# State-space outputs copied out of their PSUM banks by ScalarE, both in one step, and retention's offsets made by GpSimd

## The chip, the cores and the metric

The kernel runs on one core of one Trainium2 chip. The metric is the device time in microseconds (us) of one execution: the kernel before was run three times, and one further execution was recorded by the hardware profiler. Its rows are what the prediction reads. PE is TensorE (the matrix engine), ACT is ScalarE, DVE is VectorE, POOL is GpSimd, SP is SyncE, which issues most transfers.

## The reference

A trunk of two layers runs on two groups of 1024 tokens with 1024 channels. Layer 0 is the one that the change touches. One input projection feeds retention heads and state-space (S5) groups side by side; each is gated, and one output projection follows:

```python
z = h @ w_in
q, k, v, ga, ub, gb = jnp.split(z, [...], axis=-1)
o_a = _head_norm(_retention(q, k, v.reshape(hs))).reshape(B, L, D_RET) * jax.nn.silu(ga)
...
def _head_norm(o):
    mu = jnp.mean(of, axis=-1, keepdims=True)
    var = jnp.mean(jnp.square(of - mu), axis=-1, keepdims=True)
    return ((of - mu) * lax.rsqrt(var + EPS)).astype(o.dtype)
...
def _s5(u, ...):                     # 32 groups of 16 channels, 64 complex states each
    y = _s5_scan(... forward) + _s5_scan(... backward)
    y = y.reshape(B, L, D_SSM) + d_skip.astype(jnp.float32) * uf
    y = jax.nn.gelu(y)
    y = y * jax.nn.sigmoid(y @ w_glu.astype(jnp.float32))
```

Layer 1 is neighbourhood attention with its own projections. The change does not touch it.

## The kernel before

Every projection is made from matrices split into a high and a low part, so that one product takes three matmuls (wh·hh, wh·hl, wl·hh; `dense`, L259). `project` (L238) walks over column blocks of the weights in two halves of 512 tokens, 24 matmuls each, into bank d of PSUM. After each half it calls `unit()` (L183), which lets every background task take one step: the S5 task (`s5`, L824), one retention task per head and group (`ret_mix`, L972), and others. TensorE's instructions keep the order in which the program issues them, so the projection's matmuls fill the time between the small matmuls of the tasks. The order on the other engines is set by the framework's scheduler, and then each engine works its list off in order.

PSUM has eight banks here (L1367): two for d, and one each for a, b, c, z, y and e. A bank is written again only when the last reader of what it held is done.

S5 runs in 16 rounds, one per pair of groups g0 and g1, with four steps each (L839 to L857). Step 1: `s5_states` of g0 (four matmuls into bank z; two DVE products L790 and L791, a POOL sum L792, four DVE scans L795, two DVE products L796 and L797, a POOL sum L798), the output of the last pair's g1, and `s5_begin` of the next pair (POOL, L688 and following). Step 2: `s5_states` of g1. Step 3: `s5_place` of g0 (two ACT copies of the scanned states into `xs`) and `s5_tables` of the next pair (DVE). Step 4: `s5_place` of g1, `s5_matrices` of the next pair (PE into banks e and z, ACT copies), and the output of g0.

An output (`s5_out`, L807) is three matmuls into bank y and then the first form of gelu: ACT squares the bank into y2 (L816), DVE makes (y2 + 1)·y (L817, reads the bank), ACT takes the tanh (L818), DVE makes (tanh + 1)·y into g2 (L820, reads the bank again), and two stores take g2 away. So bank y is held from the first matmul to the end of L820, and g0 of a pair and g1 of it use it in neighbouring steps.

A retention head's `outputs` (L1016) sums into bank b (or another), takes mean and variance on DVE, makes the inverse root brs in two instructions (`rsqrt`: DVE L206, POOL L207, a power), and then the offset bnb = -mean·brs on DVE (L1034). One step later `normal` (L1037) runs four ACT activations (L1040) with brs as scale and bnb as offset into `on`, `finish` transposes it, multiplies by the gate (L1048) and stores it to oD. In the memory map, region A8 has one slot for `on` and one for `sd` (the scores times the decay, which `outputs` uses up).

## Time and profile before

| | us |
|---|---|
| median of 3 runs (lowest to highest) | 2236.64 (2235.96 to 2238.22) |
| the profiled execution's own time | 2242.2 |
| its span, first to last instruction | 2240.4 |
| PE, DVE, ACT, POOL busy in it | 2175.2, 1307.2, 962.3, 752.0 |

S5 and retention are active from about 150 to 900 us of the span, the output projection of layer 0 follows to about 1112 us, then layer 1. The mean granted TensorE clock is 0.988 of full. A row of the trace names line, engine, operation, output and inputs; "[2.07 <-DVE E L820]" means that the engine sat idle for 2.07 us and that the DVE instruction of line 820, which writes to region E, ended that. A name such as psy is bank y, E and A are regions of SBUF.

### The profile page before, as it was taken

The page shows a single profiled execution, that of the slowest core. Times are in us where ns is not written, and L with a number is a line of the kernel's source. Part 1 is how long each engine was busy: PE and PEld are TensorE (multiplying, and loading weights), DVE is VectorE, ACT ScalarE, POOL GpSimd, SP SyncE. Part 2 cuts the span into 40 slices and gives each one's busy share as a digit, 9 for nine tenths or more (in the row PEclk, how much of TensorE's full clock was granted, in tenths as well). Part 3 has the DMA queues.
Part 4 walks back from the last instruction along what each step waited for, and adds up shares of the span by engine and source line. Part 5 has one row for each costly group of instructions (what it writes and reads, how often), then busy time and mean ns, then how long its engine had stood idle before and what let it go on. Part 6 is the DMA issues. An engine that isn't in the chain of part 4 may idle for free.

```text
span 2240.4 us, 35109 instructions
## 1 busy us (share of the span) xinstructions
PE 2175.2 (97%) x13248; PEld 1830.9 (82%) x13248; DVE 1307.2 (58%) x2865; ACT 962.3 (43%) x2114; POOL 752.0 (34%) x646
## 2 busy tenths in 40 slices
PE   7999999998999999999999999999999999999998
PEld 4668778876878888888989898888888898987886
DVE  4736777878787556475434545457555555457322
ACT  4634434434443444243344444447444445355211
POOL 2544355557464120355611111113111212113333
PEclk9999999999999999999999999999999999999999
DMA  9993322224212245535521112124111111115454
GB/s 333 287 272 95 92 75 46 71 72 125 67 56 59 83 148 172 177 129 169 163 69 52 51 40 63 45 69 100 55 55 50 45 55 55 55 41 159 113 139 123
DMA packets 292640, 231.12 MB, mean 103 GB/s; under 512 B 54392, under 2 KB 263672, under 8 KB 292472
## 3 DMA queue, kind: packets, MB, share of 16 engines
q1 hardware_dynamic: 289016, 220.51, 33.2%
q10 hardware_dynamic: 3456, 8.39, 1.0%
q8 instruction: 104, 1.70, 0.3%
q14 instruction: 64, 0.52, 0.1%
HBM read 169.92 MB, written 56.84 MB: 101 GB/s over the span
## 4 chain that ended last, share of the span: by engine, by line
PE 77%; DVE 8%; DMA 7%; POOL 3%; issue 3%; ACT 3%; SPq 1%; DVEq 0%; ACTq 0%; POOLq 0%
PE psd L131 56%; PE psc L131 5%; PE psa L131 5%; PE psb L136 4%; DMA out_y<-h_lo 4%; PE psb L131 2%; PE psz L131 2%; DVE E L795 2%; PE psy L131 2%; DMA oD<-A 1%; PE psa L136 1%; DMA wr<-in_w_in_ab 1%; ACT h_hi L202 1%; DVE A L688 1%; PE pse L131 1%
## 5 line engine op out<-in xcount | busy, mean ns | idle before, releaser
L131 PE MATMUL psd<-h_hi,wh 128*128 128x512 f32 x1392 | 554.1, 398 | 3.0 <-DVE A L879 3.0
L131 PE MATMUL psd<-h_lo,wh 128*128 128x512 f32 x1392 | 547.3, 393 | 0.6 <-DVE h_lo L476 0.4
L131 PE MATMUL psd<-h_hi,wl 128*128 128x512 f32 x1392 | 545.6, 392 | 0.0
L131 PEld LDWEIGHTS psd<-h_hi,wh 128*128 128x128 f32 x1392 | 263.2, 189 | 59.3 <-DVE A L879 3.5
L131 PEld LDWEIGHTS psd<-h_hi,wl 128*128 128x128 f32 x1392 | 262.7, 189 | 55.9 <-issue 0.4
L131 PEld LDWEIGHTS psd<-h_lo,wh 128*128 128x128 f32 x1392 | 263.0, 189 | 55.4 <-issue 2.9
L131 PE MATMUL psd<-wh,h_hi 128*128 128x256 f32 (+1 forms) x960 | 279.5, 304 | 3.0 <-DVE A L946 2.0
L131 PE MATMUL psd<-wl,h_hi 128*128 128x256 f32 (+1 forms) x864 | 251.3, 291 | 0.1
L202 ACT ACTIVATE wh<-wr 128x1024 fp32r<-128x1024 f32 x118 | 124.7, 1058 | 244.6 <-PE psd L131 132.6
L213 POOL TENSOR_TENSOR wl<-wr,wh 128x1024 fp32r<-128x1024 f32 x51 | 126.5, 2480 | 262.3 <-ACT wh L202 230.3
L131 PE MATMUL psd<-wh,h_lo 128*128 128x256 f32 x768 | 213.7, 278 | 0.0
L131 PEld LDWEIGHTS psd<-wh,h_hi 128*128 128x128 f32 x960 | 181.0, 189 | 12.0 <-DVE A L946 2.4
L131 PEld LDWEIGHTS psd<-wl,h_hi 128*128 128x128 f32 x864 | 162.6, 188 | 3.9 <-POOL wl L213 0.5
L1236 POOL TENSOR_TENSOR A<-A,A 128x256 f32<-128x256 f32 (+1 forms) x80 | 56.5, 727 | 264.7 <-DVE nm L1254 260.0
L131 PEld LDWEIGHTS psd<-wh,h_lo 128*128 128x128 f32 x768 | 145.0, 189 | 0.3
L213 DVE TENSOR_TENSOR wl<-wr,wh 128x1024 fp32r<-128x1024 f32 x67 | 87.4, 1306 | 72.2 <-ACT wh L202 72.1
L1256 ACT ACTIVATE E<-E,nm 128x368 f32<-128x368 f32 (+1 forms) x172 | 98.0, 571 | 52.0 <-DVE nm L1254 51.8
L395 DVE TENSOR_TENSOR rs<-ss 128x1 f32<-128x1 f32 x64 | 42.2, 660 | 116.5 <-ACT h_lo L1153 56.4
L1274 DVE COPY A<-psb 128x384 f32<-128x384 f32 x64 | 33.5, 523 | 122.5 <-PE psb L136 121.3
L688 POOL TENSOR_TENSOR A<-A 128x288 f32<-128x288 f32 (+1 forms) x128 | 92.8, 745 | 30.9 <-DVE E L736 22.1
L131 PE MATMUL psd<-ow,oh 128*128 128x512 f32 x320 | 101.4, 396 | 1.0 <-ACT oh L202 1.0
L1236 POOL TENSOR_TENSOR A<-A 128x368 f32<-128x368 f32 x16 | 13.9, 891 | 254.3 <-DVE nm L1254 253.7
(351 smaller groups left out, 4409.7 us busy)
## 6 DMA issues: line engine op xcount, KB each, us to landing
wr<-in_w_in_c SPq DMA_DIRECT2D x64, 512.0 KB
wr<-in_w_in_ab SPq DMA_DIRECT2D x48, 512.0 KB
wr<-oD SPq DMA_DIRECT2D x32, 512.0 KB
wn<-in_w_mod SPq DMA_DIRECT2D x24, 512.0 KB
wm<-in_w_mod SPq DMA_DIRECT2D x8, 1024.0 KB
ox<-in_x SPq DMA_DIRECT2D x16, 512.0 KB
x1D<-ox SPq DMA_DIRECT2D x16, 512.0 KB
oD<-E SPq DMA_DIRECT2D x32, 256.0 KB
```

Source lines behind the costliest of these rows:

```text
L131: i = self.nc.tensor.matmul(*a, **k)
L136: i = self.nc.tensor.transpose(*a, **k)
L202: self.nc.scalar.activation(dst, src, AF.Copy, scale=scale)
L213: e.tensor_tensor(lo, raw, hi.bitcast(F32), SUB)
L395: self.nc.vector.tensor_tensor(rs, ss[:, 0:1], ss[:, 1:2], ADD)
L688: eng.tensor_tensor(dst, x.unsqueeze(3).to_broadcast(sh), y.unsqueeze(2).to_broadcast(sh), op)
L795: Vv.tensor_tensor_scan(t1[:, q], r8, t1[:, q], 0.0, MUL, ADD)
L1236: self.nc.gpsimd.tensor_tensor(b, raw[a][:, c0:c0 + n], mask, ADD)
L1256: nc.scalar.activation(sn, sn, AF.Exp, bias=nm, scale=-1.0, accum_out=su)
L1274: self.nc.vector.tensor_copy(pt, pp)
```

## The change

- **The memory map.** A8 holds two slots of `sd`. `on` is gone: `outputs` hands its `sd` on, and `normal` writes over it.
- **S5's outputs.** After the square (now L818) ACT also copies the bank into g2 (`copy_a`, L202; yc is a view of g2). Both DVE products, L820 (in place of L817) and L827 (in place of L820), read SBUF alone. g0's output goes to bank y and g1's to bank e. Both outputs of a pair are issued in step 1 of the next round, and the new `s5_gelu` (tanh L826, second product L827, stores) in step 2. The loop has a 17th, partial round for the last pair.
- **Placing.** Both `s5_place` calls stand in step 4 (g0's stood in step 3), and the copies into bm moved from `s5_tables` (step 3) to `s5_matrices` (step 4).
- **Retention's offset.** DVE makes bnb = -mean (L1047) before the root, and POOL multiplies it by brs (L1049) after the power.

```diff
-    "A7 qf 2048 qb 2048; A8 sd 2048 on 2048; A9 vfb 2048 th 2048; A10 rt1 2048 rt2 2048")
+    "A7 qf 2048 qb 2048; A8 sd 2048 sd 2048; A9 vfb 2048 th 2048; A10 rt1 2048 rt2 2048")
...
     def s5_out(self, st, g):
-        x, gi = self.xs[g], 2 * st["pi"] + g
-        ys = self.pst("y")[:, 0:256]
+        x = self.xs[g]
+        ys = self.pst("ye"[g])[:, 0:256]
...
         y2 = self.t([P, 256], "y2")
+        g2 = self.t([P, 2, P], "g2")
+        yc = g2.rearrange("p s c -> p (s c)")
         nc.scalar.activation(y2, ys, AF.Square, scale=0.044715 ** 0.5)
-        Vv.scalar_tensor_tensor(y2, y2, 1.0, ys, ADD, MUL)
+        self.copy_a(yc, ys)
+        Vv.scalar_tensor_tensor(y2, y2, 1.0, yc, ADD, MUL)
+        st["y"][g] = y2, g2, yc
+
+    def s5_gelu(self, st, g):
+        nc, Vv, gi = self.nc, self.nc.vector, 2 * st["pi"] + g
+        y2, g2, yc = st["y"][g]
         nc.scalar.activation(y2, y2, AF.Tanh, scale=G0)
-        g2 = self.t([P, 2, P], "g2")
-        Vv.scalar_tensor_tensor(g2.rearrange("p s c -> p (s c)"), y2, 1.0, ys, ADD, MUL)
+        Vv.scalar_tensor_tensor(yc, y2, 1.0, yc, ADD, MUL)
...
-        for pi in range(16):
-            self.s5_states(st, 0)
-            if pi:
-                self.s5_out(last, 1)
+        last = None
+        for pi in range(17):
+            if st:
+                self.s5_states(st, 0)
+            if last:
+                for g in range(2):
+                    self.s5_out(last, g)
             nx = self.s5_begin(pi + 1) if pi < 15 else None
             yield
-            self.s5_states(st, 1)
+            if st:
+                self.s5_states(st, 1)
+            if last:
+                for g in range(2):
+                    self.s5_gelu(last, g)
+            if not st:
+                return
             yield
-            self.s5_place(st, 0)
             if nx:
                 self.s5_tables(nx)
             yield
-            self.s5_place(st, 1)
+            for g in range(2):
+                self.s5_place(st, g)
             if nx:
                 self.s5_matrices(nx)
-            self.s5_out(st, 0)
             last, st = st, nx
             yield
-        self.s5_out(last, 1)
...
+            Vv.tensor_scalar(nb, mv[:, :, 0], -1.0, None, MUL)
             self.rsqrt(rs, mv[:, :, 1], 4, 1.0, EPS)
-            Vv.scalar_tensor_tensor(nb, mv[:, :, 0], -1.0, rs, MUL, MUL)
-            return po3, rs, nb
-
-        def normal(po3, rs, nb):
-            on = self.t([P, 4, P], "on")
+            G.tensor_tensor(nb, nb, rs, MUL)
+            return po3, rs, nb, sd
+
+        def normal(po3, rs, nb, on):
```

Three places show how the lists of the engines move. On TensorE, step 4 of the first round before (psy_1797 is the output of g0, from the states placed just ahead; pse_1768 and psz_1774 are the next pair's matrices):

```order
L136 MATMUL pse_1768<-ident,E_183_1345 128x128 x4
L131 MATMUL psz_1774<-A_192_1397,A_184_1346 48x144 x2
L131 MATMUL psz_1774<-A_184_1346 48x144 x2
L131 MATMUL psy_1797<-E_193_1410,E_198_1454 128x256
L131 MATMUL psy_1797<-E_183_1345,A_192_1397 128x256
L131 MATMUL psy_1797<-E_183_1345,A_184_1346 128x256
L131 MATMUL pse_1807<-sel,A_191_1395 128x2
```

and step 1 of the next round in the changed kernel (psz_1854 are the states of the next pair's g0; psy_1869 and pse_1876 are the outputs of g0 and g1):

```order
L131 MATMUL psz_1854<-E_193_1410 64x256 x4
L131 MATMUL psy_1869<-E_193_1410,E_198_1454 128x256
L131 MATMUL psy_1869<-E_183_1345,A_192_1397 128x256
L131 MATMUL psy_1869<-E_183_1345,A_184_1346 128x256
L131 MATMUL pse_1876<-E_193_1410,E_198_1454 128x256
L131 MATMUL pse_1876<-E_183_1345,A_192_1397 128x256
L131 MATMUL pse_1876<-E_183_1345,A_184_1346 128x256
L131 MATMUL pse_1900<-wr_1724,cs 32x128 x8
L136 MATMUL psa_1915<-ident,kT_1570 128x128 x4
```

The three matmuls of g0's output moved from behind psz's matrices to behind psz's states, a step later; the three of g1's output kept their place and changed their bank. Nothing else moved on TensorE.

On ScalarE, the same place about the fourth round (psb_2998 in the first list and psb_3000 in the second are the same retention output). Before:

```order
L816 ACTIVATE A_184_1346<-psy_2961 128x256
L202 ACTIVATE A_191_1395<-pse_2988 128x128
L818 ACTIVATE A_184_1346<-A_184_1346 128x256
L202 ACTIVATE wh_3051<-wr_3050 128x1024
L202 ACTIVATE A_213_1571<-psd_3025 64x512 x2
L202 ACTIVATE E_183_1345<-E_217_1595 64x4x127 x2
L1040 ACTIVATE A_257_2086<-psb_2998,bnb_3013,brs_3012 128x128 x4
```

and now:

```order
L818 ACTIVATE E_198_1454<-psy_2959 128x256
L202 ACTIVATE E_198_1454<-psy_2959 128x256
L818 ACTIVATE A_184_1346<-pse_2966 128x256
L202 ACTIVATE E_198_1454<-pse_2966 128x256
L826 ACTIVATE E_198_1454<-E_198_1454 128x256
L202 ACTIVATE A_191_1395<-pse_2990 128x128
L826 ACTIVATE A_184_1346<-A_184_1346 128x256
L202 ACTIVATE E_183_1345<-E_217_1595 64x4x127 x2
L202 ACTIVATE wh_3054<-wr_3053 128x1024
L202 ACTIVATE A_213_1571<-psd_3028 64x512 x2
L1054 ACTIVATE A_257_2084<-psb_3000,bnb_3015,brs_3014 128x128 x4
```

Two squares with a copy each stand together, the two tanh follow with one copy between them, and the copies of scanned states (E_183) moved ahead of the weight cast wh; the four activations of the normalisation stand behind all of these in both lists.

On VectorE, that retention output's statistics and offset. Before (L1034 is the offset, L790 and L791 the next state products):

```order
L797 TENSOR_TENSOR E_217_1595<-E_217_1595,E_198_1454 128x512
L1032 BN_AGGR bmv_3011<-bst_3010 128x2 x4
L206 TENSOR_SCALAR brs_3012<-bmv_3011 128x4
L790 TENSOR_TENSOR E_217_1595<-psz_3061,E_198_1454 128x512
L791 TENSOR_TENSOR E_217_1595<-psz_3061,E_183_1345 128x512
L371 TENSOR_TENSOR mods<-pse_3076,bmod 128x2
L1034 SCALAR_TENSOR_TENSOR bnb_3013<-bmv_3011,brs_3012 128x4
L946 TENSOR_TENSOR A_213_1571<-psd_3025,cosT_1538 128x512
L947 TENSOR_TENSOR A_213_1571<-A_213_1571,sinT_1540 128x512
```

and now (L1047 is -mean):

```order
L827 SCALAR_TENSOR_TENSOR E_198_1454<-E_198_1454 128x256
L796 TENSOR_TENSOR E_217_1595<-E_217_1595,E_183_1345 128x512
L827 SCALAR_TENSOR_TENSOR E_198_1454<-A_184_1346,E_198_1454 128x256
L797 TENSOR_TENSOR E_217_1595<-E_217_1595,E_198_1454 128x512
L1045 BN_STATS bst_3012<-psb_3000 128x6 x4
L1046 BN_AGGR bmv_3013<-bst_3012 128x2 x4
L1047 TENSOR_SCALAR bnb_3015<-bmv_3013 128x4
L206 TENSOR_SCALAR brs_3014<-bmv_3013 128x4
L790 TENSOR_TENSOR E_217_1595<-psz_3064,E_198_1454 128x512
```

The offset is gone from behind L790, L791 and L371; -mean stands directly ahead of the root's first half. On GpSimd the product has come in behind the power, here with two of `s5_begin`'s products between:

```order
L715 TENSOR_TENSOR E_183_1345<-A_191_1395,A_192_1397 128x2x128
L207 TENSOR_TENSOR brs_3014<-brs_3014,mhalf 128x4
L688 TENSOR_TENSOR A_191_1395<-A_191_1395 128x256
L688 TENSOR_TENSOR A_192_1397<-A_191_1395 128x256
L1049 TENSOR_TENSOR bnb_3015<-bnb_3015,brs_3014 128x4
L213 TENSOR_TENSOR wl_3055<-wr_3053,wh_3054 128x1024
```

Of the 16 products of this kind (L1049), 12 follow their power directly, 3 have two L688 between and one has L715 and L213 between.

## Rows read from the trace of the kernel before

**Rows 1.** The page, part 1: busy time, share of the span and instructions of each engine

```profile
PE 2175.2 (97%) x13248; PEld 1830.9 (82%) x13248; DVE 1307.2 (58%) x2865; ACT 962.3 (43%) x2114; POOL 752.0 (34%) x646
```

**Rows 2.** The windows: us, busy per engine (x instructions), PEclk, DMA share, GB/s

```profile
500.00:600.00 100.00, 89.37 (x527) 73.63 (x526) 80.65 (x120) 50.44 (x109) 64.16 (x59) 0.98 0.32 95
...
1000.00:2000.00 1000.00, 999.80 (x6508) 870.20 (x6507) 531.64 (x1331) 448.81 (x1005) 228.30 (x187) 1.00 0.24 69
...
361.00:369.00 8.00, 5.93 (x25) 4.69 (x26) 4.75 (x9) 3.07 (x10) 4.38 (x6) 0.65 0.08 18
...
716.00:722.00 6.00, 4.17 (x17) 3.21 (x14) 2.95 (x6) 2.14 (x6) 3.24 (x3) 0.72 0.13 31
```

**Rows 3.** TensorE's waits from 190 to 900: us in total, times, longest us

```profile
PE psy L131 <- DVE E L820: 8.9, 5, 3.4
PE psa L131 <- DVE qT L948: 5.9, 2, 3.5
...
PE psz L131 <- ACT k L202: 3.5, 3, 1.9
PE pse L131 <- ACT E L202: 3.1, 2, 2.9
PE psd L131 <- DVE A L879: 3.0, 1, 3.0
```

**Rows 4.** TensorE's timeline: start, us, instruction [idle before it <-what ended it]

```profile
364.11 1.19 PE L131 MATMUL psy<-E,E 128*128 128x256 f32 x2 [2.07 <-DVE E L820]
...
369.22 0.56 PE L131 MATMUL psd<-wh,h_hi 128*128 128x256 f32 x1
...
542.85 0.67 PE L131 MATMUL psy<-E,E 128*128 128x256 f32 x2 [3.36 <-DVE E L820]
...
718.18 1.02 PE L131 MATMUL psy<-E,E 128*128 128x256 f32 x2 [1.83 <-DVE E L820]
...
720.70 1.06 PE L136 MATMUL psc<-ident,A 128*128 128x128 f32 x4
...
823.12 2.09 PE L131 MATMUL psz<-ghl,gw 128*128 128x256 f32 x12 [2.20 <-ACT A L933]
```

**Rows 5.** ScalarE's timeline at three places, same columns

```profile
269.37 1.50 ACT L1040 ACTIVATE A<-psb,bnb,brs 128x128 f32<-128x128 f32 x4 [1.62 <-DVE bnb L1034]
...
356.31 0.46 ACT L1040 ACTIVATE A<-psb,bnb,brs 128x128 f32<-128x128 f32 x1 [2.08 <-DMA oD<-A]
...
821.29 1.50 ACT L1040 ACTIVATE A<-psb,bnb,brs 128x128 f32<-128x128 f32 x4 [4.22 <-DVE bnb L1034]
```

**Rows 6.** VectorE's timeline at 819, same columns

```profile
818.91 2.34 DVE L1034 SCALAR_TENSOR_TENSOR bnb<-bmv,brs 128x4 f32<-128x4 f32 x1 [3.46 <-POOL brs L207]
```

**Rows 7.** VectorE's groups from 150 to 900: busy us, mean ns | idle before, releaser

```profile
L688 DVE TENSOR_TENSOR A<-A 128x256 f32<-128x256 f32 x64 | 42.6, 704 | 12.9 <-POOL E L715 12.6
...
L733 DVE TENSOR_TENSOR E<-A,A 128x256 f32<-128x256 f32 x16 | 9.5, 596 | 0.2
...
L1034 DVE SCALAR_TENSOR_TENSOR bnb<-bmv,brs 128x4 f32<-128x4 f32 x16 | 8.7, 545 | 16.2 <-POOL brs L207 16.2
...
L736 DVE TENSOR_TENSOR E<-A,A 128x256 f32<-128x256 f32 x16 | 6.7, 419 | 0.3
...
L817 DVE SCALAR_TENSOR_TENSOR A<-A,psy 128x256 f32<-128x256 f32 x16 | 6.6, 412 | 3.2 <-ACT A L816 3.2
```

**Rows 8.** GpSimd's groups of the same stretch, same columns

```profile
L688 POOL TENSOR_TENSOR A<-A 128x256 f32<-128x256 f32 x64 | 42.9, 691 | 1.9
L213 POOL TENSOR_TENSOR wl<-wr,wh 128x1024 fp32r<-128x1024 f32 x14 | 35.5, 2539 | 41.4 <-ACT wh L202 41.4
...
L207 POOL TENSOR_TENSOR brs<-brs,mhalf 128x4 f32<-128x4 f32 x16 | 17.8, 1114 | 70.1 <-DVE brs L206 70.0
```

**Rows 9.** ScalarE's groups of the same stretch, same columns

```profile
L1040 ACT ACTIVATE A<-psb,bnb,brs 128x128 f32<-128x128 f32 x64 | 24.2, 456 | 55.6 <-DVE bnb L1034 50.3 <-PE psd L131 3.1 <-DMA oD<-A 2.1
...
L816 ACT ACTIVATE A<-psy 128x256 f32<-128x256 f32 x16 | 6.1, 383 | 18.6 <-PE psy L131 18.5
```

More of the change, by code (lines that the diff above doesn't have):

```diff
@@ L720, in s5_begin @@
                 self.load(u[:, g, s], self.uD[s][gi * 16:gi * 16 + 16].rearrange("i t c -> t i c"))
-        return dict(pi=pi, pp=pp, car=car, cai=cai, ep=ep, u=u, x=[None, None])
+        return dict(pi=pi, pp=pp, car=car, cai=cai, ep=ep, u=u, x=[None, None], y=[None, None])
     def s5_tables(self, st):
@@ L738, in s5_tables, with s5_matrices @@
         st.update(cos=cos, sn=sn)
+    def s5_matrices(self, st):
+        nc, Vv, pi = self.nc, self.nc.vector, st["pi"]
         for d in range(2):
@@ L742, in s5_tables @@
                         st["pp"][rows, 0:64].rearrange("p (r g i) -> p g r i", r=2, g=2))
-    def s5_matrices(self, st):
-        nc, Vv, pi = self.nc, self.nc.vector, st["pi"]
         pev = self.pst("e").rearrange("p (g r x) -> p g r x", g=2, r=2)
```

## The prediction

> **What bounds the kernel now.** The page comes first: TensorE is busy for 97% of the span, the next engine (VectorE) for 58% [rows 1]. The windows then say where the missing 3% are. From 1000 to 2000 us TensorE is busy for 999.80 of 1000 us, so nothing can be won there; from 500 to 600 us it is busy for 89.37 of 100, with VectorE at 80.65 and ScalarE at 50.44 [rows 2]. All the room lies in the S5 and retention stretch. The third view, TensorE's waits between 190 and 900 us, names what it waits for: five waits of 8.9 us in all for L820, which frees bank y; 5.9 us for retention's rotated q (L948) and 3.0 us for L879, both on VectorE; 3.5 us and 3.1 us for ScalarE's copies (L202) of k and E [rows 3]. So VectorE is the engine that TensorE meets most often, ScalarE the second. The timeline shows a second cost: after a wait the matmuls run slowly. The granted clock has two levels, 1.2 and 2.4 GHz; its mean, as a share of the upper one, is 0.65 from 361 to 369 us and 0.72 from 716 to 722 us [rows 2], around two of the waits for L820 [rows 4], and 1.00 from 1000 to 2000 us.
>
> **Term 1, the banks.** Each output held bank y through square, L817, tanh and L820; now ScalarE's square and copy free it. Two outputs no longer meet in one bank in neighbouring steps either, since g1 has bank e. The five waits for L820 go: -8.9 us [rows 3]. Behind the wait at 364.11 the small matmuls take until 369.22, 5.11 us, and behind the one at 718.18 until 720.70, 2.52 us [rows 4]. At 2.4 GHz, twice the low level, they would take half of that, so 2.6 and 1.3 us go as well if the engine no longer idles there (an estimate). Term 1: -12.8 us. What is late next behind these waits are the projection's evacuations on VectorE (L948, L879).
>
> **Term 2, retention's offsets.** L1034 waited 16.2 us in all for POOL's power, holding VectorE's list behind it [rows 7], and ScalarE's L1040 waited 50.3 us for L1034, with all its later copies queued behind it [rows 9]. Most of this is waiting for the statistics and hidden. It shows on TensorE at two places. At 818.91 L1034 came 3.46 us after VectorE had nothing else to do and then took 2.34 us [rows 6]; ScalarE's L1040 began only at 821.29, and TensorE waited 2.20 us, to 823.12, for the ScalarE copy queued behind it [rows 4, 5]. With the product right behind the power on POOL the copy comes about 2 us earlier: -2.2 us. At 269.37 L1040 waited 1.62 us for L1034 [rows 5], and ScalarE's E copy, for which TensorE waits (longest 2.9 us [rows 3]), stands behind it: -1.5 us. Term 2: -3.7 us. That -mean becomes an instruction of its own on VectorE costs nothing: it replaces L1034 one for one and waits for no other engine.
>
> **Term 3, two slots for sd.** At 356.31 ScalarE waited 2.08 us for a store out of the only `on` slot [rows 5]; the wait of 1.9 us for k that follows on TensorE [rows 3] is released by copies queued behind it. -1.9 us. The gross gain is 18.4 us.
>
> **What comes back.** (a) TensorE that arrives earlier meets VectorE earlier. In the window from 500 to 600 us VectorE is at 80.65%, and the longest wait for L820 (3.36 us, at 542.85 [rows 4]) lies there; besides the three shown the other two come to 8.9 - 3.36 - 2.07 - 1.83 = 1.6 us. I take half of 3.36 + 1.6 as returned: +2.5 us; the bounds are 0 and all the 8.9 us. (b) ScalarE gets 32 copies of 128x256 out of PSUM. The nearest row is its own square of the same tile, 0.383 us [rows 9]: 12.3 us on an engine that is half idle in this stretch. At most all of it delays a copy that TensorE waits for, at least none; I take 2.0 us, since the waits for ScalarE in rows 3 are few. (c) The 64 products L820 and L827 now take both inputs from SBUF. With one input in PSUM L817 takes 412 ns; of the same shape with both in SBUF L736 takes 419 ns, L733 596 and L688 704 [rows 7]. So each costs between 0.007 and 0.292 us more, 0.4 to 18.7 us on VectorE. L736 and L733 are the nearest, S5's own products; between them lies 0.095 us, 6.1 us in all. VectorE saves the 16.2 us of waiting at L1034, which covers most of it; I put a third on the path, +2.0 us. With L736's price (c) would be nothing and the sum below -13.4 us; with L688's, all of it on the path, (c) would be 18.7 us and the sum +5.3 us. (d) The 16 products on POOL have no row. The same shape takes 0.545 us on VectorE and POOL's power 1.114 us [rows 7, 8], 8.7 to 17.8 us on an engine that is at 64.16% at most in the window shown. Twelve follow their power directly; three have two L688 (0.691 us each) and one an L715 and an L213 (2.539 us) ahead [rows 8], so ScalarE's L1040 gets those no earlier than now, and the price of that is +0.5 us. (e) Placing both groups in step 4, the bm copies a step later and the tanh in step 2 delay nothing that I can see: the outputs are now issued one step after placing, behind four state matmuls, and g2's stores feed a read-back long after S5's end. If that cover fails, the last output costs one step at the most.
>
> The sum is -18.4 + 2.5 + 2.0 + 2.0 + 0.5 = -11.4 us: the profiled execution would go from 2242.2 to 2230.8. That execution is 5.6 us above the median of 2236.64, so I forecast **2225 us**. About 0.2% (4.5 us) is what a measurement of this kernel can tell from no change.
>
> **Why two inputs in SBUF may cost more.** L1034 is 128x4 with both inputs in SBUF; its mean is 545 ns, and at 818.91 it took 2.34 us [rows 6, 7], close to POOL's split L213 of 2.539 us [rows 8]. L817, one input in PSUM, has a mean of 412 ns over 16. The Trainium skill, page "SBUF — State Buffer", section "Who interferes with whom", states the rule: "A DVE instruction with two SBUF inputs contends with a GpSimd instruction that reads SBUF". The trace agrees. By that rule every one of the 64 products becomes exposed, and POOL's sums too; it speaks against this change and is the first rival below.
>
> **Rivals.** *Slower: the products on VectorE are blocked by POOL.* If each of the 64 is stretched as L733 is (0.184 us, 11.8 us in all), all of it reaches TensorE and the whole 8.9 us of (a) come back: -18.4 + 8.9 + 2.0 + 11.8 + 0.5 = +4.8, 2241.4 us; with L688's 0.292 us +11.7, 2248 us. It decides from 7.0 us on that reach TensorE, 0.11 us per product. For it: VectorE above 80% and POOL at 64% in the same window. Against it: L736 hardly stretches, and VectorE is no longer held at L1034 and for the tanh. Chance 0.14.
> *No change: VectorE is the bound and the waits only move.* All 8.9 us of (a) come back at L948 and L879, ScalarE's copies cost 4 and the products 3 us: -18.4 + 8.9 + 4 + 3 + 0.5 = -2.0, 2234.6 us. For it: TensorE waits as long for L948 and L879 (8.9 us) as for L820. The case that the change doesn't do what it says belongs here: bank e also serves the next pair's matrices, whose copy could hold g1's output. But the state matmuls ahead of it need that same copy, so it is no new wait. Chance 0.19 together.
> *The full gain.* Nothing of (a) comes back, and VectorE, with 16.2 us less waiting, also halves the 8.9 us for L948 and L879: -18.4 - 4.4 + 1 = -21.8, 2214.8 us. For it: the waits for L820 are spread over 16 rounds with long projections between. Chance 0.20.
>
> **The numbers.** The forecast has a chance of 0.47, its own range 2217 to 2232 us by the bounds of (a) to (c). The range that should hold 8 in 10 takes in most of the full gain and of the slower case: 2210 to 2242 us. Faster by over 0.2% means below 2232.2 us: forecast and full gain, 0.67. Within 0.2%: 0.19. Slower, above 2241.1 us: 0.14.
>
> **What would show it.** Right: no wait of TensorE for L820 or L827; the waits psy and pse, if any, for ScalarE's L202; L1040 near 819 instead of 821 us; TensorE above 92% from 500 to 600 us. Wrong: waits for L948, L879 or L790 above 15 us together (VectorE is the bound); L820 and L827 with a mean over 550 ns and POOL's L798 longer (the slower rival); new waits of TensorE for copies behind L818, L202 and L1054 on ScalarE; the product L1049 over 1.2 us with L1054 waiting for it.

## The result and the profile after

The changed kernel takes 2255.55 us (median of 4 runs, 2246.89 to 2258.74) against 2237.43 us (4 runs, 2235.96 to 2238.61): a ratio of 1.0072, 95% interval 1.0046 to 1.0098. It is slower by some 16 us by the ratio (the medians lie 18 us apart), where 2225 us were forecast. Its profiled execution took 2256.26 us, 14 us more than that of before.

The page, part 1, of the changed kernel, to be held against [rows 1]:

```profile
PE 2181.6 (97%) x13248; PEld 1837.6 (82%) x13248; DVE 1312.6 (58%) x2865; ACT 972.8 (43%) x2146; POOL 751.4 (33%) x662
```

TensorE does the same 13248 matmuls in 6.4 us more busy time; its span grew by 14.1 us (2240.4 to 2254.5), so the other 7.7 us are idle time. The window from 500 to 600 us tells where the busy time comes from [rows 2]:

```profile
500.00:600.00 100.00, 89.06 (x463) 72.11 (x463) 78.68 (x122) 43.60 (x92) 62.43 (x60) 0.91 0.34 102
```

463 matmuls instead of 527 in the same 100 us (in part other ones, since the changed kernel is late by then), at a mean granted clock of 0.91 instead of 0.98: more of the stretch is spent at 1.2 GHz. The loss is made ahead of 910 us: behind that the kernels go at one pace, and TensorE is busy for 587.72 us of the 590 from 910 to 1500 us in both. TensorE's waits from 150 to 910 us in the changed kernel answer to [rows 3]:

```profile
PE psa L131 <- DVE qT L962: 11.6, 3, 4.3
PE pse L131 <- ACT E L202: 9.1, 8, 1.7
PE psz L131 <- ACT k L202: 4.9, 2, 3.5
PE psd L131 <- DVE A L893: 4.8, 2, 2.9
PE psd L131 <- DVE A L960: 4.8, 1, 4.8
PE psa L136 <- ACT A L1054: 2.5, 1, 2.5
PE psz L131 <- ACT A L947: 1.9, 2, 1.6
PE psb L131 <- DVE A L1027: 0.3, 1, 0.3
```

The change does what it says: no wait for a product of S5's outputs is left. In their place stand eight waits for bank e (9.1 us; before there were two, 3.1 us), and the waits for VectorE's rotation, L960 to L962 (L946 to L948 before), went from 7.9 to 16.4 us. Two places of TensorE's timeline show the two kinds, and a third the longest wait:

```profile
216.00 0.64 PE L131 MATMUL pse<-wr,cs 128*32 128x128 f32 x16 [1.73 <-ACT E L202]
...
462.81 1.65 PE L131 MATMUL psa<-qT,kT 128*128 128x128 f32 x8 [4.26 <-DVE qT L962]
...
581.65 0.58 PE L131 MATMUL psd<-wh,h_hi 128*128 128x256 f32 x1 [4.76 <-DVE A L960]
```

**The first kind.** pse<-wr and pse<-sel are the modulation blocks of layer 1, a background task that uses bank e in the first five rounds. In step 1 they follow g1's output, which now fills bank e, and wait until ScalarE has squared and copied it (four waits, 0.75 to 1.73 us). In step 4 they follow the next pair's matrices in bank e; g0's output used to stand between the two and covered ScalarE's copy of the matrices.

**The second kind.** VectorE's timeline ahead of the wait at 462.81:

```profile
454.19 0.28 DVE L1009 COPY stf<-psc 128x128 f32<-128x128 f32 x1
456.68 3.99 DVE L688 TENSOR_TENSOR A<-A 128x256 f32<-128x256 f32 x2 [2.21 <-POOL E L715]
460.59 0.68 DVE L960 TENSOR_TENSOR A<-psd,cosT 128x512 f32<-128x512 f32 x1
461.19 0.68 DVE L961 TENSOR_TENSOR A<-A,sinT 128x512 f32<-128x512 f32 x1
...
461.98 0.68 DVE L962 TENSOR_TENSOR qT<-A 128x512 f32<-128x512 f32 x1
```

GpSimd's timeline at the same time:

```profile
453.79 0.74 POOL L715 TENSOR_TENSOR E<-A,A 128x256 f32<-128x256 f32 x1
454.61 1.21 POOL L688 TENSOR_TENSOR A<-A 128x256 f32<-128x256 f32 x2
455.90 0.74 POOL L715 TENSOR_TENSOR E<-A,A 128x256 f32<-128x256 f32 x1
456.60 2.38 POOL L213 TENSOR_TENSOR wl<-wr,wh 128x1024 fp32r<-128x1024 f32 x1
458.94 1.44 POOL L792 TENSOR_TENSOR E<-E 128x512 f32<-128x512 f32 x1
```

And ScalarE's:

```profile
453.87 1.27 ACT L202 ACTIVATE E<-E 64x508 f32<-64x508 f32 x2 [2.82 <-POOL E L798]
455.16 1.06 ACT L202 ACTIVATE wh<-wr 128x1024 fp32r<-128x1024 f32 x1
456.25 1.21 ACT L202 ACTIVATE A<-psd 64x512 f32<-64x512 f32 x2
```

VectorE stands idle for 2.21 us at L688 (the next pair's tables), which waits for GpSimd's L715; then its two L688 take 3.99 us while GpSimd runs L213 and L792; and only then comes the rotation that TensorE waits for, although ScalarE's copies for it were done at 457.46. The copies in turn stand behind the placed states (E<-E), which wait for GpSimd's L798. In the kernel before, VectorE's list at this place has rotation first and no L688 ahead of it:

```profile
446.24 0.68 DVE L1048 SCALAR_TENSOR_TENSOR A<-psa,ga 128x512 f32<-128x512 f32 x1
446.84 0.68 DVE L946 TENSOR_TENSOR A<-psd,cosT 128x512 f32<-128x512 f32 x1
447.44 1.02 DVE L947 TENSOR_TENSOR A<-A,sinT 128x512 f32<-128x512 f32 x1
...
448.58 0.91 DVE L948 TENSOR_TENSOR qT<-A 128x512 f32<-128x512 f32 x1
```

VectorE's groups of the changed kernel from 150 to 920 us answer to [rows 7]:

```profile
L688 DVE TENSOR_TENSOR A<-A 128x256 f32<-128x256 f32 x64 | 48.6, 796 | 26.4 <-POOL E L715 26.1
...
L820 DVE SCALAR_TENSOR_TENSOR E<-E 128x256 f32<-128x256 f32 x16 | 14.0, 877 | 7.9 <-ACT E L202 7.9
...
L820 DVE SCALAR_TENSOR_TENSOR A<-A,E 128x256 f32<-128x256 f32 x16 | 11.2, 701 | 0.0
...
L827 DVE SCALAR_TENSOR_TENSOR E<-E 128x256 f32<-128x256 f32 x16 | 10.8, 674 | 1.0 <-ACT E L826 1.0
...
L827 DVE SCALAR_TENSOR_TENSOR E<-A,E 128x256 f32<-128x256 f32 x16 | 7.7, 480 | 0.0
```

L688's waiting grew from 12.9 to 26.4 us. The products of S5's outputs, now with both inputs in SBUF, take 43.7 us together; at the 412 ns of before 64 of them would take 26.4. GpSimd's new product costs little:

```profile
L1049 POOL TENSOR_TENSOR bnb<-bnb,brs 128x4 f32<-128x4 f32 x16 | 4.0, 247 | 0.9
```

### The profile page after: what moved, and what is told of

The parts are those of the page before. It is cut to its first block, busy times and chain, and to the rows that moved or that the text cites. A ratio compares the mean times of both kernels' runs of the same rounds, so it can differ in the third digit from the quotient of the medians.

```text
span 2254.5 us, 35172 instructions
## 1 busy us (share of the span) xinstructions
PE 2181.6 (97%) x13248; PEld 1837.6 (82%) x13248; DVE 1312.6 (58%) x2865; ACT 972.8 (43%) x2146; POOL 751.4 (33%) x662
## 4 chain that ended last, share of the span: by engine, by line
PE 82%; DVE 8%; ACT 3%; DMA 2%; POOL 2%; issue 2%; SPq 0%; ACTq 0%; DVEq 0%; POOLq 0%
PE psd L131 62%; PE psc L131 5%; PE psa L131 5%; PE psb L136 4%; PE psz L131 2%; PE psb L131 2%; DVE E L795 2%; PE psy L131 1%; PE pse L131 1%; DVE A L688 1%; PE psa L136 1%; DMA wr<-in_w_in_ab 1%; ACT E L202 1%; DMA wn<-in_w_mod 1%; POOL A L688 0%
## 5 line engine op out<-in xcount | busy, mean ns | idle before, releaser
L202 ACT ACTIVATE wh<-wr 128x1024 fp32r<-128x1024 f32 x118 | 124.9, 1058 | 229.8 <-PE psd L131 124.1
L213 POOL TENSOR_TENSOR wl<-wr,wh 128x1024 fp32r<-128x1024 f32 x51 | 127.5, 2499 | 265.4 <-ACT wh L202 233.4
L213 DVE TENSOR_TENSOR wl<-wr,wh 128x1024 fp32r<-128x1024 f32 x67 | 86.7, 1295 | 73.9 <-ACT wh L202 73.8
L688 POOL TENSOR_TENSOR A<-A 128x288 f32<-128x288 f32 (+1 forms) x128 | 90.6, 727 | 33.9 <-DVE E L736 19.7
```

Of the source, the lines that this page charges most:

```text
L202: self.nc.scalar.activation(dst, src, AF.Copy, scale=scale)
L213: e.tensor_tensor(lo, raw, hi.bitcast(F32), SUB)
L688: eng.tensor_tensor(dst, x.unsqueeze(3).to_broadcast(sh), y.unsqueeze(2).to_broadcast(sh), op)
```

## Theories and experiments

A: bank e, shared with the modulation blocks. B: the stretched products on VectorE. C: two outputs crowded into one step. D: the offset's product on GpSimd. E: the moved placing of g0. F: the order of VectorE's list, L688 ahead of rotation. The ratios, each to runs of the kernel before on the same chip, in the order of the argument:

| kernel | median us | ratio | 95% interval |
|---|---|---|---|
| changed kernel | 2255.55 | 1.0072 | 1.0046 to 1.0098 |
| retention part alone | 2230.64 | 0.9959 | 0.9946 to 0.9972 |
| two slots of sd alone | 2238.13 | 1.0004 | 0.9996 to 1.0013 |
| changed, offset on VectorE | 2255.54 | 1.0075 | 1.0062 to 1.0088 |
| changed, banks swapped | 2256.80 | 1.0077 | 1.0064 to 1.0091 |
| changed, modulation blocks in y | 2249.56 | 1.0048 | 1.0030 to 1.0065 |
| changed, L820 from the bank | 2266.16 | 1.0117 | 1.0104 to 1.0130 |
| both outputs in step 1, no copy | 2259.65 | 1.0101 | 1.0087 to 1.0116 |
| copy alone | 2241.07 | 1.0014 | 1.0005 to 1.0023 |
| retention, copy, late half; g0 in step 4 | 2237.93 | 0.9999 | 0.9988 to 1.0010 |
| changed, g0's placing back | 2256.13 | 1.0077 | 1.0061 to 1.0093 |
| changed, two lists held | 2259.75 | 1.0096 | 1.0079 to 1.0112 |
| retention, two lists held | 2236.18 | 0.9989 | 0.9979 to 0.9999 |
| changed, rotation first | 2237.82 | 0.9997 | 0.9988 to 1.0006 |
| changed, rotation first, blocks in y | 2228.25 | 0.9959 | 0.9945 to 0.9973 |
| retention, rotation first | 2228.24 | 0.9953 | 0.9940 to 0.9966 |
| retention, g1 in e after the blocks | 2227.77 | 0.9956 | 0.9944 to 0.9968 |
| the same, rotation first | 2221.90 | 0.9925 | 0.9911 to 0.9939 |

**1. The retention part alone.** On the kernel before, only the map's line and the lines of `outputs` and `normal`:

```diff
-            Vv.scalar_tensor_tensor(nb, mv[:, :, 0], -1.0, rs, MUL, MUL)
-            return po3, rs, nb
+            G.tensor_tensor(nb, nb, rs, MUL)
+            return po3, rs, nb, sd
```

> The kernel before with the retention part of the change alone: two slots of sd, the offset's product on POOL. My prediction's terms 2 and 3 gave it -5.6 us at most: a ratio of 0.9975 to 1.000 to the kernel before, the wait at 823 us gone and ScalarE's wait for a store out of the on slot gone. Theory D: slower than the kernel before by 3 us or more. Theories A to C: at or below the kernel before, since the loss is made by S5's part.

Measured: 0.9959, some 9 us faster and more than the 5.6 us expected. So S5's part loses some 25 us in the changed kernel, and D falls. The largest step comes near 355 us. ScalarE's timeline of this kernel there, against 356.31 in [rows 5]:

```profile
354.66 0.60 ACT L202 ACTIVATE E<-pse 128x512 f32<-128x512 f32 x1
...
356.71 1.51 ACT L1040 ACTIVATE A<-psb,bnb,brs 128x128 f32<-128x128 f32 x4
```

The normalisation now stands behind the copies of E and k in the list, where before it stood ahead of them and held them; TensorE's waits for k and for bank y at this place (1.89 and 2.07 us) are gone.

**2. The two slots alone.**

```diff
-A8 sd 2048 on 2048;
+A8 sd 2048 sd 2048;
```

> The kernel before with two slots of sd alone, the normalisation written over sd, the offset on VectorE as before. The retention part alone gave 0.9959, and 5 us of it came at one place, near 350 us, where the waits for k and for bank y went. If that is the slots' (term 3, in which the wait of ScalarE for the store out of the on slot holds the copies behind it), this kernel takes 4 to 7 us less than before and lacks the 2.5 us that came at 820 us; if it is the offset's, this stays within 2 us of before.

Measured: 1.0004, within 2 us of before. ScalarE no longer waits for the store there, but 1.01 us for the offset instead. So the slots alone don't make the gain of 1; it needs the offset's product on GpSimd. Whether that needs the second slot too wasn't run.

**3. The offset back on VectorE in the changed kernel** (the first diff, reversed).

> The changed kernel with retention's offset made by VectorE again, in one instruction behind POOL's power; S5's outputs and the two slots of sd stay as changed. If the offset's product on POOL is what loses (theory D: ScalarE's normalisation waited 64.9 us for it, against 50.3 us for L1034 before), the time falls by 5 us or more and the waits for copies behind the normalisation go. If it helped as predicted, the time rises by about 3 to 4 us and a wait of some 2 us comes back near 830 us, where the normalisation holds the gate's copies. Theories A to C: the S5 part alone makes the loss, so this stays 10 to 20 us above the kernel before.

Measured: 1.0075, no different from the changed kernel. D falls again, but so does an expectation: with S5's part in, the offset's 10 us don't show at all. A wait of 2.43 us came back at 839 us, as expected; others went.

**4. The banks swapped.**

```diff
-        ys = self.pst("ye"[g])[:, 0:256]
+        ys = self.pst("ey"[g])[:, 0:256]
```

> The changed kernel with the two outputs' banks swapped: g0's output goes to e, g1's to y, so that ScalarE frees e by the time of three matmuls and one copy earlier. Theory A (the changed kernel loses in bank e, which the modulation blocks use right behind g1's output: seven new waits pse<-L202 of 8.9 us and the low clock behind them): the seven waits fall to under 4 us, and the time falls by 4 to 9 us against the changed kernel, to a ratio of about 1.003 to 1.006 to the kernel before. Theory B (it loses on VectorE, whose products with two SBUF inputs are stretched) and C (it loses because both outputs crowd VectorE's list in one step and hold its later work): no change in time beyond 2 us, the VectorE waits (L962, L893, L960, 21.2 us in the changed kernel) stay.

Measured: 1.0077, no gain. The four waits of step 1 went, but those of step 4 stayed, and at 276 us one of them grew from 1.70 to 4.58 us; the wait for qT near 312 us grew from 2.95 to 4.55. This run doesn't decide on A.

**5. The first product from the bank.**

```diff
-        Vv.scalar_tensor_tensor(y2, y2, 1.0, yc, ADD, MUL)
+        Vv.scalar_tensor_tensor(y2, y2, 1.0, ys, ADD, MUL)
```

> The changed kernel with the first product (L820) reading the bank again instead of ScalarE's copy; the copy and all else stay. Theory B: L820's mean falls from 877 and 701 ns to about 412, VectorE is relieved of some 12 us, its waits on TensorE's side fall by about a third (21.2 to 14 us) and the time by 5 to 8 us. Theory A: the banks are now held until L820 has run, so the waits for banks e and y grow above 8.9 us and the time does not fall or rises by up to 8 us. Theory C: no change beyond 3 us.

Measured: 1.0117. The modulation blocks now wait for L820: four waits of 4.5 to 5.2 us, 19.5 us in all. This is A's side, and at some 10 us above the changed kernel a little more than the 8 us it allowed; it shows what ScalarE's copy is good for in this schedule. It doesn't price B: the products' stretch fell (415 and 400 ns), but the waits for bank e grew by more.

**6. Both outputs in step 1 without copy and without delay** (square, products and tanh straight from banks y and e, placing as changed but the outputs' second half not moved). On the changed kernel, in `s5_out`, with the rest of `s5_gelu` following at once:

```diff
-        self.copy_a(yc, ys)
-        Vv.scalar_tensor_tensor(y2, y2, 1.0, yc, ADD, MUL)
+        Vv.scalar_tensor_tensor(y2, y2, 1.0, ys, ADD, MUL)
...
-        Vv.scalar_tensor_tensor(yc, y2, 1.0, yc, ADD, MUL)
+        Vv.scalar_tensor_tensor(g2.rearrange("p s c -> p (s c)"), y2, 1.0, ys, ADD, MUL)
...
-                    self.s5_gelu(last, g)
```

> The changed kernel without the copy and without the delayed second half: both outputs in step 1, g0 in bank y and g1 in e, square, products and tanh all in that step straight from the banks; placing and bm copies as changed; retention as changed. Theories C and E (the moved steps lose): still above the kernel before, ratio 1.004 to 1.012. Theory B (the copy and its products lose): at or below the kernel before, 0.995 to 1.000, with the products at some 412 ns. Theory A: bank e is now held until the second product, so the waits of the modulation blocks for it grow to over 15 us by 350 us, as in the run with the first product from the bank.

Measured: 1.0101, with four waits of 5.0 to 6.5 us for bank e (the view names no releaser for them, but they stand at the same matmuls, pse<-wr, as those of run 5). The stretched products are not needed for a loss: without them it is larger. How much they cost can't be read here, since bank e is also held longer. The wait of 3.31 us for qT behind L688 is there too.

**7. The copy alone** on the kernel before (steps and banks as before).

```diff
         nc.scalar.activation(y2, ys, AF.Square, scale=0.044715 ** 0.5)
-        Vv.scalar_tensor_tensor(y2, y2, 1.0, ys, ADD, MUL)
+        self.copy_a(yc, ys)
+        Vv.scalar_tensor_tensor(y2, y2, 1.0, yc, ADD, MUL)
...
-        Vv.scalar_tensor_tensor(g2.rearrange("p s c -> p (s c)"), y2, 1.0, ys, ADD, MUL)
+        Vv.scalar_tensor_tensor(yc, y2, 1.0, yc, ADD, MUL)
```

> The kernel before with ScalarE's copy alone: the output is copied into g2 behind the square, both products read SBUF, and nothing is moved between steps or banks. My prediction's term 1 would show here: the waits psy<-L820 of 8.9 us go and the time falls by 5 to 13 us (ratio 0.994 to 0.998). Theory B (stretched products lose): L817's and L820's mean rises from some 412 to 600 to 800 ns, and the time is at or above the kernel before (ratio 1.000 to 1.006). Theories A, C and E: faster, as term 1 says, since banks, steps and placing are as before.

Measured: 1.0014. The five waits for bank y are gone; the first rows of its waits show what came:

```profile
PE psa L131 <- DVE qT L950: 7.2, 2, 4.0
PE psd L131 <- DVE A L948: 5.2, 2, 4.1
PE psd L131 <- DVE A L881: 4.1, 1, 4.1
```

10.9 us of these waits before (5.9, 2.0 and 3.0), 16.5 us now. One of the two groups of first products took 1126 ns on the mean, another 479. The bank's gain came back at VectorE and a little more, as B says of this part; 1.0014 lies near the lower end of B's 1.000 to 1.006.

**8. g0's placing back in step 3.**

```diff
+            self.s5_place(st, 0)
             if nx:
                 self.s5_tables(nx)
             yield
-            for g in range(2):
-                self.s5_place(st, g)
+            self.s5_place(st, 1)
```

> The changed kernel with the placing of g0 back in step 3, as before the change; all else as changed. Theory E (the moved placing changes the lists: ScalarE's copies of scanned states, which wait for GpSimd's L798, now stand ahead of the weight cast and of the copies of rotated q and k, and VectorE's L688 ahead of L960 to L962, so that TensorE waits for qT at 312, 463 and 679 us, 11.6 us, and for L960 at 582 us, 4.8 us): those four waits fall to the 7.9 us of before or less, and the time falls by 6 to 12 us, to a ratio of 1.002 to 1.005. Theory A (bank e) and theory B (products with two inputs from SBUF): no more than 3 us. If only the clumping of two outputs in one step does it (theory C): no more than 3 us.

Measured: 1.0077, and the waits are those of the changed kernel (11.6 us for qT, 9.1 for bank e, 5.0 for L960). At the wait of 4.28 us for qT, now near 455 us, VectorE's list is the same too: 2.21 us idle, 3.99 us of L688, then rotation. E falls: the order there does not depend on where placing is issued.

**9. Retention, copy and late half, with g0's output left in step 4 and both in bank y.**

```diff
             if pi:
                 self.s5_out(last, 1)
+                self.s5_gelu(last, 0)
...
             self.s5_states(st, 1)
+            if pi:
+                self.s5_gelu(last, 1)
             yield
```

> The retention part, the copy and the second half a step later, but g0's output stays in step 4 and both in bank y, as before; placing and bm as before. The lists of ScalarE and VectorE stand in the order of before around rotation. If the loss is in moving g0's output to step 1 (bank e and the lists, theories A and F): between the retention part alone and the copy alone, ratio 0.994 to 0.999. If the late half or the copy loses (theory B): 1.003 or more. The waits psy<-L820 are gone in either case.

Measured: 0.9999, between what either side expected. Against the changed kernel 0.7% are won by steps and banks as before (g0 in step 4, bank y alone, placing and bm where they were); against the retention part alone 0.4% are lost by copy and late half. So the copy with its products is not free, even where nothing else is moved.

**10. The modulation blocks in bank y.**

```diff
-            pa = self.pst("e")[:, 0:P]
+            pa = self.pst("y")[:, 0:P]
...
-            p2 = self.pst("e")[:, 0:2]
+            p2 = self.pst("y")[:, 0:2]
```

> The changed kernel with the modulation blocks' matmuls in bank y instead of e; y is idle in step 4 and freed some 0.8 us earlier than e in step 1. Theory A: the eight waits pse<-L202 of 9.1 us shrink to under 2 us, and the time falls by 5 to 9 us (ratio 1.003 to 1.005) if nothing takes their place; if VectorE is what TensorE meets next (theory F), the lag is back by 320 us at the wait for qT, and the time falls by less than 3 us.

Measured: 1.0048. All eight waits for bank e are gone, and the median is 6 us lower; but the interval overlaps that of the changed kernel, so the size is not sure from this pair alone (run 12 has a clear one). A holds, for a smaller part of the loss. The waits for qT (13.2 us) and L960 (6.2 us) remain.

**11. Two lists held in program order**, ScalarE's copies for rotation and placing, VectorE's rotation and L688:

```diff
-        self.copy_a(t2[0:64], ps[64:128])
-        self.copy_a(t2[64:128], ps[0:64])
-        nc.vector.tensor_tensor(t1, ps, self.cosT[:, sl], MUL)
+        self.copy_a(t2[0:64], ps[64:128], pin=True)
+        self.copy_a(t2[64:128], ps[0:64], pin=True)
+        self.tc.keep_in_program_order(nc.vector.tensor_tensor(t1, ps, self.cosT[:, sl], MUL))
...
```

> The changed kernel with the lists' order held: ScalarE's copies for rotation and for placing, and VectorE's rotation and L688, keep the order in which the program issues them, so that rotation stands ahead of the tables' L688 and its copies ahead of the placed states. Theory F (with both outputs in step 1 the framework's lists put placing, which waits for GpSimd's L798, ahead of the rotation's copies, and L688 ahead of rotation; TensorE waits for qT at 463 and 312 us and for L960): the waits for qT and L960, 16.4 us in the changed kernel, fall under 8 us, the time by 5 to 12 us, ratio 0.999 to 1.005. Theory A (bank e): the pse waits stay and the time falls by less than 3 us. It can also turn out slower, if the tables or the placing now come too late for the next round; then waits for psz and psy show it.

> The control for the pinned lists: the kernel before with the retention part and the same two lists held in program order. Its lists already had rotation ahead of placing at the places in question, so theory F expects no more than 3 us between it and the retention part alone (ratio 0.994 to 0.998); if holding the order is a gain or a loss by itself, it shows here and is taken off the reading of the pinned changed kernel.

Measured: 1.0096 for the changed kernel, 0.9989 for the control. The waits for qT and L960 fell to 4.2 us, but the waits for copies out of banks e and z grew from 9.1 to 19.8 and from 4.9 to 10.8 us. Holding ScalarE's list costs in both kernels, so this pair can't tell whether VectorE's order is the cause.

**12. VectorE's order alone** (rotation's three instructions and L688; ScalarE's list is left to the scheduler), in the changed kernel with the blocks in y, in the changed kernel itself, and in the retention part alone as the control.

```diff
-        nc.vector.tensor_tensor(t1, ps, self.cosT[:, sl], MUL)
+        self.tc.keep_in_program_order(nc.vector.tensor_tensor(t1, ps, self.cosT[:, sl], MUL))
...
-        eng.tensor_tensor(dst, x.unsqueeze(3).to_broadcast(sh), y.unsqueeze(2).to_broadcast(sh), op)
+        (self.tc.keep_in_program_order if eng is self.nc.vector else id)(eng.tensor_tensor(dst, x.unsqueeze(3).to_broadcast(sh), y.unsqueeze(2).to_broadcast(sh), op))
```

> The changed kernel with the modulation blocks in bank y and, on VectorE alone, rotation and L688 held in program order, so that rotation is no longer queued behind L688, which waits for GpSimd's L715. Theory F (order of VectorE's list): the waits for qT, 13.2 us with the blocks in y, fall to 4 to 8 us and the lag against the kernel before does not jump by 5 us at 460 us; the ratio falls from 1.0048 to 1.000 to 1.003. If the waits only change their names (VectorE's and ScalarE's work of that stretch is late as a whole), waits for psz and pse behind ScalarE's copies take their place and the ratio stays at 1.004 or above.

> The changed kernel as it is, with bank e still shared with the modulation blocks, and VectorE's rotation and L688 held in program order. Theory F with the size that the run with the blocks in y showed (20 us): ratio 0.998 to 1.001, the eight pse waits of 9.1 us still there, the waits for qT and L960 under 10 us (16.4 us in the changed kernel). If both repairs are needed together, it stays above 1.004.

> The control: the kernel before with the retention part and VectorE's rotation and L688 held in program order. If holding that order is a gain for any S5 schedule, the ratio falls from 0.9959 by as much as it did for the changed kernel (0.9 points, to some 0.987). If it only puts right what the changed schedule had put wrong, the ratio stays at 0.994 to 0.997.

Measured: 0.9959 (lower than either side expected), 0.9997 and 0.9953. The changed kernel gains 0.75% from the order alone, some 17 us; the control gains 0.06%, nothing that its interval can tell. In the changed kernel with rotation first, VectorE's list at the place of the wait at 462.81 is:

```profile
448.42 0.69 DVE L960 TENSOR_TENSOR A<-psd,cosT 128x512 f32<-128x512 f32 x1 [3.04 <-ACT A L202]
...
450.59 1.55 DVE L962 TENSOR_TENSOR qT<-A 128x512 f32<-128x512 f32 x1
...
457.44 1.48 DVE L688 TENSOR_TENSOR A<-A 128x256 f32<-128x256 f32 x2
```

Rotation waits for ScalarE's copies alone, L688 comes behind it, and TensorE waits 2.83 us for qT instead of 4.26. TensorE's waits in this kernel:

```profile
PE pse L131 <- ACT E L202: 9.5, 8, 1.7
PE psa L131 <- DVE qT L962: 8.0, 3, 3.1
...
PE psd L131 <- DVE A L960: 1.3, 2, 1.0
```

the engines' busy times, and VectorE's L688:

```profile
PE 2171.8 (97%) x13248; PEld 1828.8 (82%) x13248; DVE 1310.4 (59%) x2865; ACT 971.6 (43%) x2146; POOL 753.5 (34%) x662
...
L688 DVE TENSOR_TENSOR A<-A 128x256 f32<-128x256 f32 x64 | 34.6, 580 | 3.9 <-POOL E L715 3.6
```

Of the 17.5 us between the two spans (2254.5 and 2237.0), TensorE's busy time gives 9.8 (2181.6 to 2171.8, the same matmuls at a mean granted clock of 0.992 instead of 0.986) and its idle time the other 7.7. Some 3 us of the 17.5 arise ahead of 293 us, where the waits of the two are the same, so they are not the order's. Busy and idle together L688 takes 38.5 us of VectorE's list there, against 75.0 in the changed kernel and 55.5 before. That alone is no price: in the control it falls from 64.4 to 40.1 us and the time stays. There TensorE's waits for VectorE's rotation shrink too, from 8.5 to 4.7 us, but those for bank y grow from 7.2 to 9.9:

```profile
PE psy L131 <- DVE E L820: 9.9, 4, 5.3
```

The products of the outputs still take 845, 676, 674 and 478 ns in the changed kernel with rotation first: B's stretch is all there and both outputs still stand in one step (C), and the loss against the kernel before is gone. What the stretch costs beside that shows only against a kernel without it whose banks are free as well (run 13).

**13. The gain that was sought, without copies.** On the retention part alone:

```diff
-        ys = self.pst("y")[:, 0:256]
+        ys = self.pst("e" if g and st["pi"] > 5 else "y")[:, 0:256]
```

and then with VectorE's order held as in 12.

> The retention part alone, and g1's output in bank e from the seventh pair on, when the modulation blocks have finished; g0's output stays in step 4, without copy and without delay. This takes what term 1 was after (two outputs in one bank in neighbouring steps) without ScalarE's copies, without products that read SBUF twice and without the collision with the modulation blocks. The four waits psy<-L820 of 7.2 us that the retention part alone still has should go; if a third to two thirds of that is kept, the ratio is 0.993 to 0.995; if VectorE is what TensorE meets next, it stays at 0.996.

> The version with retention's part and g1's output in bank e after the modulation blocks, and VectorE's rotation and L688 held in program order. In that version the banks no longer wait and TensorE meets VectorE at qT (5.9 us), L946 (5.6 us) and L879 (3.0 us). If rotation ahead of L688 shortens these waits by half, the ratio is about 0.992; if VectorE's lists were in that order already, as before the change, it stays at 0.995 to 0.996.

Measured: 0.9956 and 0.9925. In the first the waits for bank y (7.2 us) are gone and the time is the same: L946 went from 2.6 to 5.6 us and L879 stands with 3.0. The longest of these waits, 4.13 us, ends at 559.50 us, and here too VectorE's L688 stands ahead of rotation:

```profile
557.14 1.70 DVE L688 TENSOR_TENSOR A<-A 128x256 f32<-128x256 f32 x2
558.77 0.68 DVE L946 TENSOR_TENSOR A<-psd,cosT 128x512 f32<-128x512 f32 x1
```

The kernel before has the same order at this place, ahead of its own wait of 2.00 us for L946:

```profile
564.24 1.70 DVE L688 TENSOR_TENSOR A<-A 128x256 f32<-128x256 f32 x2
565.86 0.68 DVE L946 TENSOR_TENSOR A<-psd,cosT 128x512 f32<-128x512 f32 x1
```

So this order is not the changed schedule's alone. On the retention part the split wins 0.03% by itself and the held order 0.06%, neither clear of noise, but both together win 0.34%. So 0.3 of the 0.75% that the held order gives the changed kernel may be no repair of its schedule, since the split, whose S5 steps were not moved, gains as much. And the changed kernel with both repairs, 0.9959 in run 12, stays 0.34% (some 7 us) above this last one, 0.9925; both have two banks for the outputs, and rotation first. Copies, stretched products, the late half and the moved steps make that difference together; run 9 puts copies and late half at about this size. With rotation first the split wins 0.28% over the control of 12. This last kernel, 2221.90 us, beats the kernel before by 0.75% and the changed one by 1.5%. Its first waits:

```profile
PE pse L131 <- ACT E L202: 4.8, 3, 3.1
PE psa L131 <- DVE qT L948: 4.7, 2, 2.9
PE psz L131 <- ACT k L202: 3.4, 2, 2.4
```

## Why the prediction was wrong, point by point

**What failed: step (e),** put at nothing. It said that the moved steps "delay nothing that I can see"; the second rival added of bank e that "it is no new wait". The moved steps and the second bank cost two things.

First, moving g0's output out of step 4 and g1's into bank e exposed the modulation blocks. Their row (pse<-wr) stands right behind g1's output in the piece of TensorE's order ahead of the prediction. The prediction weighed bank e against the matrices alone and not against its third user. Price: the step from 0.9997 to 0.9959 with rotation first (run 12), some 8.5 us; without it 1.0072 to 1.0048, some 5 us and not clear of noise (run 10).

Second, with both outputs in step 1 the scheduler's list for VectorE put the tables' L688 ahead of rotation where it had not stood before. The price is the 0.75% of run 12, some 17 us by the medians: with rotation first the changed kernel is level with the kernel before. That the order costs this is shown; that all of it is the changed schedule's doing is not, since the split of run 13 gains 0.31% by the same hold. Why the scheduler chose this order for this schedule is not shown; placing is not the reason (run 8).

With both repaired the changed kernel stands at 0.9959, level with the control (0.9953), so the two make up S5's loss of some 25 us. They don't give the gain that was forecast: the control still waits for bank y (9.9 us), and against the split, which hardly does (1.2 us), 0.34% are missing (run 13).

**Term 1 (-12.8 us) and (a).** The waits for bank y went as said, but (a) returned all of them and not 2.5 us: in run 7 (copy alone, 1.0014) and in run 13 (split, 0.9956 after 0.9959). The upper bound that (a) named was the better value. With rotation first the split was worth 6 us (0.9953 to 0.9925). Of the clock's 3.9 us in this term nothing can be seen apart.

**Term 2 (-3.7 us)** was right in sign and too small: 0.9959 against 1.0004 is about 10 us. It came another way than worked out. Of the two places named, the wait at 823 us fell from 2.20 to 1.06 us in run 1 and the one of 2.9 us for ScalarE's E copy stayed (2.91), the normalisation ahead of it waiting 1.61 us for the offset as before; the largest part came near 355 us, through the place of the normalisation in ScalarE's list. **Term 3 (-1.9 us)** was nothing: another wait took the place of the store's (run 2). In the changed kernel the offset's gain did not show (run 3); that TensorE met VectorE there first is likely and not shown.

**(b), the copies,** were put at 2.0 us and not measured by themselves. Run 7 gives copy and products together less the bank's gain: +3 us. **(c), the products,** were put at 6.1 us on VectorE and cost 17.3 (43.7 less 26.4), near the upper bound of 18.7. As the Trainium skill's page "SBUF — State Buffer" says in "Who interferes with whom", a VectorE instruction with two SBUF inputs contends with a GpSimd instruction that reads SBUF. The trace agrees, in these products (683 ns on the mean against 412 with one input in PSUM) and in the two L688 of 3.99 us beside L213 and L792. But the rival that was built on it is not the main cause: with the stretch unchanged the loss went (run 12), and what is left for copies, products and the moves with them is the 0.34 to 0.4% of runs 9 and 13. **(d)** was over-priced: the product takes 247 ns on GpSimd, not 545 to 1114. The 545 ns were a mean that long instances such as the one of 2.34 us had raised; half of the 16 took 164 ns or less.

**The rivals.** The slower one, 2241 to 2248 us, had the sign, but at most some two thirds of the size, and it took for the cause what was the smaller part. The second, waits that only move to VectorE, is what term 1 came to. Of the signs listed, "no wait for L820 or L827" and "waits for L948, L879 or L790 above 15 us together" were both seen: 11.6 us for L962 (L948 before) and 4.8 for L893 (L879 before). The new waits behind ScalarE's copies were seen too, eight for bank e, and half of the slower rival's sign (L820 and L827 at 683 ns on the mean, but GpSimd's L798 at 1390 as before, 1388). TensorE above 92% from 500 to 600 us, a sign of being right, was not: 89.06.

## What to carry to other kernels

Where a background task shares a bank, list every user of it in program order before moving one in: the row right behind the moved one says who will wait. A moved step can also re-order the lists that a scheduler writes for the other engines, as here VectorE's, so read those lists at the places where the bottleneck engine waits, and ask for each instruction ahead of the awaited one what it waits for itself. A wait removed in front of an engine that meets a second one soon after can be worth nothing until the second is relieved: on the retention part neither the split nor the held order gave anything alone, and both together 0.34%.

## What the runs showed of the hardware that was not expected

The same waits can cost a different time in different executions. The run with g0's placing back had, in its profiled execution, the changed kernel's waits within 0.5 us in each group but one (L893: 6.4 us against 4.8), but took 2247.46 us against 2256.26, with a mean granted clock of 0.989 against 0.986; from 150 to 910 us the means are 0.98 and 0.97. One stretch shows it: between the first two waits for bank e, 1.7 us each in both, the changed kernel took 13.1 us at a mean granted clock of 0.87 (from 202.9 us) and the other 11.5 us at 1.00 (from 200.4 us). So with the same waits TensorE ran at the low level for a part of this stretch in one execution and not in the other. The four runs of the changed kernel spread over 12 us and the four of before beside them over 3, but later sets of 11 to 23 runs of the kernel before spread over 7 to 13, so the spread is no mark of the change. What decides it was not tried.
